# An expert layer's first product: 64 of 256 tokens by gathered rows and dot products on VectorE, 192 tokens left to the dense product on TensorE

## The chip, the cores and the metric

The kernel runs on one core of one Trainium2 chip. The metric is the device time of one execution in microseconds. Every time below comes from the profile, the run times or the trace of the kernel before.

## The reference, cut to what matters

Two blocks follow each other; the changed part is the last layer of the second, an expert layer ("peer") on 256 tokens of width 2048, with 16384 experts. Each of 8 heads picks 16 experts per token, so 128 (token, expert) pairs per token are wanted, out of 16384.

```python
def peer_ffn(x, wq, sub_keys, u, v):
...
        best, pos = lax.top_k(cand, PEER_TOPK)
        expert = jnp.take_along_axis(cidx, pos, axis=-1)
        gate = jax.nn.softmax(best, axis=-1)
        u_sel = u[expert]
        v_sel = v[expert]
        act = jax.nn.gelu(jnp.einsum('td,thkd->thk', xc, u_sel).astype(jnp.float32), approximate=False)
        return jnp.einsum('thk,thkd->td', (gate * act).astype(x.dtype), v_sel)
```

## The kernel before, in words

**The dense way.** The kernel gathers nothing. It multiplies all 256 tokens by all 16384 rows of `u` (the first product), applies gelu, multiplies by a dense matrix of gates that is zero for experts not picked, and multiplies the result by all of `v` (the second product). Both weight matrices, 134 MB each, stream through once.

**A chunk.** Weights come in chunks of 128 x 1024 float32 (512 KB). `split_w` loads one on SP's queue, ScalarE rounds it to its high half (`whi`, line 132), and `sub` (line 121) makes the low half (`wlo`) as the difference, on the engines that `lo_eng[0]` lists in turn. The rings hold 5 raw chunks and 4 of each half. A chunk has 8 blocks of 128 x 128. For each, `mm3` issues two matmuls: the high half against the activations' high and low halves side by side (512 columns, line 145), and the low half against the high half alone (256 columns, line 146). Four chunks make a group of 256 experts; the first product has 64 groups (`u_group`), 256 chunks, and the second (`v_group`) another 256.

**Beside the first product** run three things, called from `mid` once per chunk. `route(0)` and `route(1)` (lines 1017 to 1066, VectorE) find each token's experts and gates for 128 tokens at a time. `gate_prep` (line 1082) makes one-hot matrices on VectorE for a unit of 4 tokens, and `gate_fire` (line 1109) multiplies them on TensorE into that unit's dense gates, which go to `Gd` in DRAM; there are 64 units. After each group, ScalarE copies the cross part (line 183), VectorE adds it (line 190), and gelu goes to `staged` and to `Ad` in DRAM. `fetch` brings `Gd` and `Ad` back, and `w_make` multiplies them into the activations of the second product.

**What sets the order.** The order in which a step stands on its engine is not that of the source alone: a scheduler fixes each engine's list when the program is built, and on the chip each engine takes its list strictly in turn.

Of the kernel before, what the change touches and what calls it, by code (L numbers as in the profile page):

```python
# [18 lines left out]
T = 256  # L19
D = 2048  # L20
KT = 16
# [18 lines left out]
GATES_AT = 16  # L40
SPLIT_FROM = 62
PER_UNIT = 2.3
# [11 lines left out]
def tile_body(ctx: ExitStack, tc: tile.TileContext, xT, vec, dw, w_ccin, w_ccout, w_m1, w_m2,  # L54
              w_p, w_ki, pool_w, rel_bias, bucket, w_o, w_q, subk, w_u, w_v, out):
# [53 lines left out]
    DVE.tensor_scalar(ident, jp[:, :128], 0.0, None, op0=OP.is_equal)  # L109
    iota = const.tile([128, 128], F32, name="iota")  # L110
# [971 lines left out]
    def gate_prep(n):  # L1082

        if n >= SPLIT_FROM:
            o = [pk("oh", [128, 4, 128], F32R, tag=f"oh{i}", bufs=1) for i in range(3)]
            t = slice(4 * n, 4 * n + 4)
            ghi = pk("ghi", [128, 4], F32R, bufs=2)
            glo = pk("glo", [128, 4], bufs=2)
            ACT.activation(ghi, R[:, 2, t], AF.Copy)
            sub(DVE, glo, R[:, 2, t], ghi)  # L1090
            for i in range(4):
                t = slice(4 * n + i, 4 * n + i + 1)
                DVE.tensor_scalar(o[0][:, i], iota, R[:, 0, t], ghi.bitcast(F32)[:, i:i + 1], op0=OP.is_equal, op1=OP.mult)
                DVE.tensor_scalar(o[1][:, i], iota, R[:, 0, t], glo[:, i:i + 1], op0=OP.is_equal, op1=OP.mult)
                DVE.tensor_scalar(o[2][:, i], iota, R[:, 1, t], None, op0=OP.is_equal)
            gates[n] = o
            return
        if not spare:
            more = slot(3, [128, 8, 4, 128], name="hot")
            flat = big.rearrange("p a b -> p (a b)").rearrange("p (n a b) -> p n a b", n=4, a=4)  # L1100
            spare.extend(flat[:, i] for i in range(4))
            spare.extend(more[:, i] for i in range(8))
        o1, o2 = spare[2 * (n % 6):2 * (n % 6) + 2]
        for i in range(4):
            t = slice(4 * n + i, 4 * n + i + 1)
            DVE.tensor_scalar(o1[:, i], iota, R[:, 0, t], R[:, 2, t], op0=OP.is_equal, op1=OP.mult)
            DVE.tensor_scalar(o2[:, i], iota, R[:, 1, t], None, op0=OP.is_equal)
        gates[n] = o1, o2

    def gate_fire(n):  # L1110
        if n % 8 == 0:
            gs.append(slot(4 + n // 8 % 2, [128, 128, 32], name="gs"))
        *o1, o2 = gates.pop(n)
        ps = aux(wide4)
        for i in range(4):
            for j, a in enumerate(o1):
                PE.matmul(ps[:, i], a[:, i], o2[:, i], start=j == 0, stop=j == len(o1) - 1)  # L1117
# [6 lines left out]
    Ad = dram.tile([8, 4, 128, 4, T], F32, name="Ad")  # L1124
    staged = slot(0, [128, 4, 4, T], name="staged")
    wts, last = {}, [None]
    acc = hf
    lnf = Layer()

    def u_group(b, g, mid=None):  # L1130

        q = g // 2

        def ev(o, ps):
            v = wk("nrm", bufs=3)
            last[0] = gathered(ps, v)
            ACT.activation(staged[:, q, o % 4], v, AF.Gelu)  # L1137

        group(w_u[8 * b + g], H, ev, g, mid=mid)
        if g % 2:  # L1140
            nc.gpsimd.dma_start(Ad[b, q], staged[:, q])  # L1141

    def fetch(n):

        if not ring4:
            ring4.append(slot(3, [128, 4, 4, T], name="got"))
            ring4.append(slot(7, [128, 4, 8, 4, 32], name="gt"))
# [6 lines left out]
    def w_make(b, q):  # L1154
# [4 lines left out]
        for i in range(4):  # L1159
            w = got[:, i]  # L1160
            with tc.issue_after(last[0].ins):
                DVE.tensor_tensor(w.rearrange("p (c t) -> p c t", c=8), w.rearrange("p (c t) -> p c t", c=8),  # L1162
                                  gt[:, :, i], OP.mult)
            put_split(wts[b], 4 * q + i, w)
# [25 lines left out]
    with phase("gate"):  # L1190
        lo_eng[0] = [DVE]
        made = [0, 0]
        ripe = [0]

        def routing():
            for b in range(2):
                yield from route(b)
                yield
                yield
                route_end(b)  # L1200

        steps = routing()
        for i in range(64):
            def mid(c, i=i):
                if c in (0, 1, 2):
                    next(steps, None)
                to = int(max(0, min(64, (4 * (i - GATES_AT) + c + 1) / PER_UNIT)))
                while made[1] < ripe[0]:
                    gate_fire(made[1])
                    made[1] += 1  # L1210
                ripe[0] = made[0]
                while made[0] < to:
                    gate_prep(made[0])
                    made[0] += 1
# [53 lines left out]
def lay_out(inp):  # L1268
# [6 lines left out]
    def cols(v):  # L1275
# [27 lines left out]
    o["w_v"] = c(a["peer_v_2"][0].reshape(128, 8, 4, 4, 8, 256).transpose(1, 4, 2, 0, 3, 5))  # L1303
    return o
# [3 lines left out]
         "bucket", "w_o", "w_q", "subk", "w_u", "w_v"]  # L1308
# [16 lines left out]
```

## Time and profile before

| what | value |
|---|---|
| runs | 3055.27, 3045.81, 3044.33 us; median 3045.81 us |
| profiled execution | 3056.73 us, span 3054.9 us |
| TensorE | 2997.2 us busy, 98% of the span |
| VectorE | 2138.3 us, 70% |
| ScalarE | 1576.6 us, 52% |
| GpSimd | 458.3 us, 15% |
| DMA | 608.20 MB, 199 GB/s over the span |

A matmul's listed duration is longer than its share of TensorE's time, since matmuls are pipelined; the distance between starts is its price. A busy share is an average over stages with different limits, so each stage is read by itself.

### The profile page before, as it was taken

The page shows a single profiled execution, that of the slowest core. Times are in us where ns is not written, and L with a number is a line of the kernel's source. Part 1 is how long each engine was busy: PE and PEld are TensorE (multiplying, and loading weights), DVE is VectorE, ACT ScalarE, POOL GpSimd, SP SyncE. Part 2 cuts the span into 40 slices and gives each one's busy share as a digit, 9 for nine tenths or more (in the row PEclk, how much of TensorE's full clock was granted, in tenths as well). Part 3 has the DMA queues.
Part 4 walks back from the last instruction along what each step waited for, and adds up shares of the span by engine and source line. Part 5 has one row for each costly group of instructions (what it writes and reads, how often), then busy time and mean ns, then how long its engine had stood idle before and what let it go on. Part 6 is the DMA issues. An engine that isn't in the chain of part 4 may idle for free.

```text
span 3054.9 us, 47026 instructions
## 1 busy us (share of the span) xinstructions
PE 2997.2 (98%) x17614; PEld 2642.9 (87%) x17614; DVE 2138.3 (70%) x3892; ACT 1576.6 (52%) x2435; POOL 458.3 (15%) x554
## 2 busy tenths in 40 slices
PE   8998999999999999999999999999999999999997
PEld 7997888888888888898888888888888888888886
DVE  7997666455565876767899666666456667676765
ACT  4446554444444644565555555555555445454444
POOL 6883100000000120014400000000100000000014
PEclk9998999999999999999999999999999999999998
DMA  6443655555555555445456666666777777777663
GB/s 224 154 152 113 206 186 186 187 186 187 186 186 186 186 187 182 158 147 179 159 187 214 207 214 227 228 214 215 277 262 245 244 231 243 233 236 241 213 188 109
DMA packets 165045, 608.20 MB, mean 199 GB/s; under 512 B 18232, under 2 KB 20288, under 8 KB 163536
## 3 DMA queue, kind: packets, MB, share of 16 engines
q1 hardware_dynamic: 148992, 533.79, 52.7%
q0 software_dynamic: 15824, 71.41, 7.0%
q8 instruction: 137, 2.24, 0.3%
q14 instruction: 92, 0.75, 0.1%
HBM read 569.40 MB, written 37.24 MB: 199 GB/s over the span
## 4 chain that ended last, share of the span: by engine, by line
PE 91%; DVE 6%; POOL 1%; ACT 1%; issue 0%; DMA 0%; ACTq 0%; DVEq 0%; POOLq 0%
PE mm L145 54%; PE mm L146 28%; DVE aux L433 3%; PE aux L1117 2%; PE mm L363 2%; PE mm L820 0%; PE mm L818 0%; PE mm L819 0%; POOL hf L762 0%; DVE h L471 0%; DVE hf L1239 0%; PE mm L949 0%; PE mm L951 0%; DVE conv L440 0%; PE mm L950 0%
## 5 line engine op out<-in xcount | busy, mean ns | idle before, releaser
L145 PE MATMUL mm<-A,whi 128*128 128x512 f32 x7056 | 2484.3, 396 | 3.6 <-DVE A L121 3.4
L146 PE MATMUL mm<-A,wlo 128*128 128x256 f32 x7088 | 1986.8, 280 | 3.5 <-POOL wlo L121 1.9
L121 DVE TENSOR_TENSOR wlo<-wraw,whi 128x1024 fp32r<-128x1024 f32 x928 | 1139.8, 1233 | 783.7 <-ACT whi L132 782.7
L145 PEld LDWEIGHTS mm<-A,whi 128*128 128x128 f32 x7056 | 1324.0, 188 | 314.6 <-DVE A L121 4.2
L132 ACT ACTIVATE whi<-wraw 128x1024 fp32r<-128x1024 f32 x976 | 1029.6, 1057 | 1042.3 <-PE mm L145 767.4
L146 PEld LDWEIGHTS mm<-A,wlo 128*128 128x128 f32 x7088 | 1339.6, 189 | 4.9 <-POOL wlo L121 2.3
L183 ACT ACTIVATE cross<-mm 128x256 f32<-128x256 f32 x439 | 164.4, 374 | 89.8 <-PE mm L146 89.8
L121 POOL TENSOR_TENSOR wlo<-wraw,whi 128x1024 fp32r<-128x1024 f32 x48 | 117.7, 2463 | 56.1 <-ACT whi L132 56.0
L433 DVE SCALAR_TENSOR_TENSOR aux<-front,dwt,aux 128x256 f32<-128x256 f32 x314 | 125.1, 477 | 0.1
L1141 POOL DMA_DIRECT2D Ad<-staged x32 | 17.2, 536 | 628.2 <-ACT staged L1137 605.7
L1149 POOL DMA_DIRECT2D gt<-Gd x32 | 28.9, 904 | 499.6 <-DVE got L1162 447.4
L231 POOL TENSOR_TENSOR accq<-sq 128x256 f32<-128x256 f32 x5 | 3.9, 777 | 650.8 <-ACT sq L238 650.8
L1137 ACT ACTIVATE staged<-nrm 128x256 f32<-128x256 f32 x128 | 53.1, 415 | 90.7 <-DVE nrm L190 90.7
L363 PE MATMUL mm<-h,raw 128*128 128x256 f32 x448 | 98.0, 379 | 0.0
L190 DVE TENSOR_TENSOR nrm<-mm,cross 128x256 f32<-128x256 f32 x192 | 80.3, 418 | 22.4 <-ACT cross L183 22.4
L363 PEld LDWEIGHTS mm<-h,raw 128*128 128x128 f32 x448 | 84.8, 191 | 11.3
L1119 ACT ACTIVATE gs<-aux 128x512 f32<-128x512 f32 x64 | 72.8, 1138 | 26.8 <-PE aux L1117 26.8
L410 POOL TENSOR_TENSOR nr<-nr 128x256 f32<-128x256 f32 x106 | 78.9, 744 | 18.1 <-ACT nr L409 12.0
L145 PE MATMUL mm<-M,whi 128*128 128x512 f32 x224 | 79.3, 397 | 0.0
L231 POOL TENSOR_TENSOR accq<-sq,accq 128x256 f32<-128x256 f32 x64 | 59.5, 930 | 129.8 <-ACT sq L238 129.5
L146 PE MATMUL mm<-M,wlo 128*128 128x256 f32 x256 | 72.5, 283 | 2.6 <-DVE wlo L121 2.6
L373 PE MATMUL mm<-A,whi 128*128 128x256 f32 x224 | 65.6, 293 | 3.3 <-DVE front L382 2.3
(308 smaller groups left out, 2503.5 us busy)
## 6 DMA issues: line engine op xcount, KB each, us to landing
wraw<-w_m SPq DMA_DIRECT2D x256, 512.0 KB, 3.5
wraw<-w_u SPq DMA_DIRECT2D x256, 512.0 KB, 3.7
wraw<-w_v SPq DMA_DIRECT2D x256, 512.0 KB, 4.3
wraw<-w_p SPq DMA_DIRECT2D x80, 512.0 KB, 3.5
wraw<-w_ccin SPq DMA_DIRECT2D x36, 512.0 KB, 3.6
wraw<-w_ccout SPq DMA_DIRECT2D x32, 512.0 KB, 4.2
wraw<-w_o SPq DMA_DIRECT2D x32, 512.0 KB, 4.3
wraw<-w_q SPq DMA_DIRECT2D x32, 512.0 KB, 3.6
```

Of the source, the lines that this page charges most:

```text
L121: return eng.tensor_tensor(out_, a, b, OP.subtract)
L132: ACT.activation(hi[:, :, :m], raw[:, :, :m], AF.Copy)
L145: PE.matmul(ps, hi[:, k, cs], a, start=kt == 0, stop=False)
L146: PE.matmul(ps[:, :T], lo[:, k, cs], a[:, 0], start=False, stop=kt == KT - 1)
L183: ACT.activation(c, ps[:, T:], AF.Copy)
L190: return DVE.tensor_tensor(dst, ps[:, :T], c, OP.add)
L231: POOL.tensor_tensor(d, ap, self.acc[k], OP.add)
L363: PE.matmul(hold[j][:, :T], raws[c][:, k, blk(j)], src[:, kt], start=kt == 0, stop=kt == KT - 1)
L373: PE.matmul(d, hi[:, k, blk(j)], a[:, 0], start=kt == 0, stop=False)
L410: POOL.tensor_tensor(t, t, p, OP.add)
L433: DVE.scalar_tensor_tensor(d, a, b, add, op0=OP.mult, op1=OP.add)
L1119: ACT.activation(gs[-1][:, :, t:t + 4].rearrange("p c t -> p t c"), ps, AF.Copy)
```

## The change

The first 64 tokens leave the dense product. The selected rows of `u` (a second copy of the weights, `u_rows`, as half rows of 1024 floats) are fetched by indirect DMA from GpSimd's queue, 128 half rows (512 KB) at a time: the two halves of one row of each of 64 tokens. Each fetch is multiplied on VectorE by the tokens' own activations (`Hx`) and summed in one instruction (`dot_rows`). There are 128 fetches and 128 dot products. `weigh` adds the two halves by a matmul, applies gelu and multiplies the gates, so that the dense gates of these tokens hold gate times activation. The dense product runs on 192 tokens: 384 and 192 columns instead of 512 and 256. `gate_prep` uses three instructions of 128 x 512 instead of eight of 128 x 128. And `lo_eng[0]` becomes [DVE, POOL] for both products, so every second chunk's low half is made on GpSimd.

```diff
     def gate_prep(n):
...
+        i = 2 * (len(order) % 2)
+        o1, o2 = (big.rearrange("p a b -> p (a b)")[:, 512 * j:512 * j + 512].rearrange("p (t a) -> p t a", t=4)
+                  for j in (i, i + 1))
+        order.append(n)
+        r = [R[:, c, 4 * n:4 * n + 4, None].to_broadcast(wide4) for c in range(3)]
+        keys = iota[:, None, :].to_broadcast(wide4)
+        DVE.tensor_tensor(o1, keys, r[0], OP.is_equal)
+        DVE.tensor_tensor(o1, o1, r[2], OP.mult)
+        DVE.tensor_tensor(o2, keys, r[1], OP.is_equal)
         gates[n] = o1, o2
...
+    def fetch_rows(j):
...
+        p = pieces[j % 5]
+        got_rows[j] = p
+        POOL.indirect_dma_start(out=p, out_offset=None, in_=u_rows,
+                                in_offset=bass.IndirectOffsetOnAxis(ap=idx[:, j:j + 1], axis=0))
+
+    def dot_rows(j):
+        p = got_rows.pop(j)
+        DVE.tensor_tensor_reduce(out=p, in0=p, in1=Hx, scale=1.0, scalar=0.0, op0=OP.mult, op1=OP.add,
+                                 accum_out=dots[:, j:j + 1])
...
+    def mm_late(ps, hi, lo, k, o, A, kt, fine):
+        a = A[kt // 8][:, kt % 8]
+        PE.matmul(ps[:, :2 * ND].rearrange("p (i t) -> p i t", i=2), hi[:, k, blk(o)], a[:, :, NS:],
+                  start=kt == 0, stop=False)
+        PE.matmul(ps[:, :ND], lo[:, k, blk(o)], a[:, 0, NS:], start=False, stop=kt == KT - 1)
...
     with phase("gate"):
-        lo_eng[0] = [DVE]
+        lo_eng[0] = [DVE, POOL]
...
+        def looking(to):
+            while looked[1] < min(to, 128):
+                dot_rows(looked[1])
+                looked[1] += 1
+                while looked[0] < min(128, looked[1] + 5):
+                    fetch_rows(looked[0])
+                    looked[0] += 1
+            if looked[1] == 128 and not done:
+                done.append(1)
+                weigh()
...
             u_group(i // 8, i % 8, mid)
-            if i == 55:
+            if i == 60:
                 for n in range(4):
                     fetch(n)
-            if i > 55 and i % 2:
-                w_make(0, (i - 56) // 2)
+            if i > 60:
+                w_make(0, i - 61)
+        w_make(0, 3)
```

**Where instructions now stand.** The first place is VectorE in the middle of `route`, with the large comparisons of its first block. `wlo` is a chunk's low half, `nrm` the addition after a group, `z` routing data. Before:

```order
L1041 TENSOR_TENSOR z_14174<-z_14173,z_14174 128x128x15
L190 TENSOR_TENSOR nrm<-mm,cross 128x256
L121 TENSOR_TENSOR wlo<-wraw,whi 128x1024 x2
L1044 TENSOR_REDUCE z_14173<-z_14174 128x128
L190 TENSOR_TENSOR nrm<-mm,cross 128x256
L121 TENSOR_TENSOR wlo<-wraw,whi 128x1024
L1046 TENSOR_TENSOR z_14174<-z_14174 128x128x15
L121 TENSOR_TENSOR wlo<-wraw,whi 128x1024 x2
```

And with the change:

```order
L1049 TENSOR_TENSOR z_14176<-z_14175,z_14176 128x128x15
L1187 TENSOR_TENSOR nrm<-mm,cross 128x192
L1052 TENSOR_REDUCE z_14175<-z_14176 128x128
L1072 TENSOR_REDUCE sm<-z_14175 128x8
L1054 TENSOR_TENSOR z_14176<-z_14176 128x128x15
L1187 TENSOR_TENSOR nrm<-mm,cross 128x192
L129 TENSOR_TENSOR wlo<-wraw,whi 128x1024
L1056 TENSOR_REDUCE z_14175<-z_14176 128x128
```

Between two low halves that VectorE makes there are more routing steps than before, and each of its low halves now stands for two chunks of the product: routing stands between the first 24 chunks, where before it was spread over some 40.

The second place is GpSimd's list during the first product. Before, it holds DMAs alone (`Ad` after every second group, `Gd` after every 8 units):

```order
L1020 CAST z_14173<-z_14173 128x256 x2
L1141 DMA Ad<-staged_15042 128x1024 x10
L1121 DMA Gd<-gs_16885 128x4096
L1141 DMA Ad<-staged_15042 128x1024 x2
L1121 DMA Gd<-gs_17471 128x4096
```

With the change, in the stretch of the dot products (`rows` and `piece` are the five buffers of fetched rows):

```order
L129 TENSOR_TENSOR wlo<-wraw,whi 128x1024
L1149 DMA rows_17127<-u_rows,z_14176 128x1024 x5
L129 TENSOR_TENSOR wlo<-wraw,whi 128x1024
L1149 DMA rows_17127<-u_rows,z_14176 128x1024 x4
L129 TENSOR_TENSOR wlo<-wraw,whi 128x1024
```

VectorE's list in the same stretch is this (the second line of each dot product reads its sum out):

```order
L129 TENSOR_TENSOR wlo<-wraw,whi 128x1024
L1154 ISA rows_17127,z_14176<-rows_17127,state_15043 128x1024
L1154 ISA z_14176 128x1
L1187 TENSOR_TENSOR nrm<-mm,cross 128x192
L1154 ISA rows_17127,z_14176<-rows_17127,state_15043 128x1024
L1154 ISA z_14176 128x1
L1187 TENSOR_TENSOR nrm<-mm,cross 128x192
L1154 ISA rows_17127,z_14176<-rows_17127,state_15043 128x1024
L1154 ISA z_14176 128x1
L1154 ISA rows_17127,z_14176<-rows_17127,state_15043 128x1024
L1154 ISA z_14176 128x1
L129 TENSOR_TENSOR wlo<-wraw,whi 128x1024
```

All 128 dot products stand between 31 low halves of VectorE, so within 62 of the 256 chunks, about four to a pair of chunks; the source asks for one in 1.3 chunks. Nearly all units of gates stand behind them.

## Rows read from the trace of the kernel before

**Rows 1.** The page's head: span, the chain's shares by engine.

```profile
span 3054.9 us, 47026 instructions
...
PE 91%; DVE 6%; POOL 1%; ACT 1%; issue 0%; DMA 0%; ACTq 0%; DVEq 0%; POOLq 0%
```

**Rows 2.** Stretches: us, busy us (x instructions) by engine, PEclk, DMA share, GB/s.

```profile
1545.00:2318.00 773.00, 773.00 (x4620) 683.89 (x4619) 544.81 (x1141) 431.97 (x600) 31.66 (x55) 1.00 0.67 227
1551.00:1670.00 119.00, 119.00 (x685) 104.29 (x684) 118.83 (x259) 63.40 (x91) 3.11 (x6) 1.00 0.64 207
2318.00:3010.00 692.00, 692.00 (x3987) 609.37 (x3986) 478.72 (x733) 344.40 (x502) 72.09 (x83) 1.00 0.70 228
```

**Rows 3.** TensorE in order of time, first product: start us, us, instruction.

```profile
1639.90 0.40 PE L145 MATMUL mm<-A,whi 128*128 128x512 f32 x1
...
1642.72 0.40 PE L145 MATMUL mm<-A,whi 128*128 128x512 f32 x1
```

**Rows 4.** TensorE in order of time: short matmuls with their own weights.

```profile
242.34 0.58 PE L244 MATMUL aux<-ones,conv 128*128 128x1 f32 x4
242.79 0.58 PE L244 MATMUL aux<-ones,sq 128*128 128x1 f32 x4
...
1804.94 1.05 PE L1117 MATMUL aux<-hot 128*128 128x128 f32 x8
1805.75 0.47 PE L145 MATMUL mm<-A,whi 128*128 128x512 f32 x1
...
2184.92 1.01 PE L1117 MATMUL aux<-oh 128*128 128x128 f32 x8
2185.76 0.45 PE L145 MATMUL mm<-A,whi 128*128 128x512 f32 x1
```

**Rows 5.** VectorE in order of time, first product.

```profile
1547.36 0.49 DVE L937 MAX8 z<-s 128x8 f32<-128x128 f32 x2 [1.49 <-ACT s L933]
...
1551.59 0.29 DVE L1024 TENSOR_TENSOR z<-z 128x128 f32<-128x128 f32 x1
...
1569.99 0.42 DVE L190 TENSOR_TENSOR nrm<-mm,cross 128x256 f32<-128x256 f32 x1
1570.33 2.35 DVE L121 TENSOR_TENSOR wlo<-wraw,whi 128x1024 fp32r<-128x1024 f32 x2
1572.60 2.14 DVE L1044 TENSOR_REDUCE z<-z 128x128 f32<-128x1920 f32 x1
```

**Rows 6.** GpSimd's low halves, all: min/median/max ns.

```profile
L121 POOL TENSOR_TENSOR wlo<-wraw,whi x48: 2349/2398/3340, 30.2 to 1532.2; 128x1024 fp32r<-128x1024 f32 x48
```

**Rows 7.** GpSimd and VectorE at once, in order of time; line 282's usual ns.

```profile
1443.74 2.44 POOL L121 TENSOR_TENSOR wlo<-wraw,whi 128x1024 fp32r<-128x1024 f32 x1 [4.84 <-ACT whi L132]
...
1443.90 2.57 DVE L282 TENSOR_TENSOR sq<-ident,t_dr 128x256 f32<-128x256 f32 x1
...
1459.49 1.21 DVE L121 TENSOR_TENSOR wlo<-wraw,whi 128x1024 fp32r<-128x1024 f32 x1
...
1459.87 3.10 POOL L121 TENSOR_TENSOR wlo<-wraw,whi 128x1024 fp32r<-128x1024 f32 x1 [1.66 <-ACT whi L132]
...
1500.83 2.49 POOL L121 TENSOR_TENSOR wlo<-wraw,whi 128x1024 fp32r<-128x1024 f32 x1 [3.87 <-ACT whi L132]
...
1501.00 0.48 DVE L937 MAX8 z<-s 128x8 f32<-128x128 f32 x2
...
L282 DVE TENSOR_TENSOR sq<-ident,t_dr x3: 425/425/2574, 246.4 to 3035.5; 128x256 f32<-128x256 f32 x3
```

**Rows 8.** A stretch at the kernel's start, columns as in the second group.

```profile
10.00:15.00 5.00, 5.00 (x17) 4.11 (x16) 4.26 (x11) 3.97 (x15) 3.11 (x7) 1.00 1.02 410
```

**Rows 9.** GpSimd's DMA issues (ns), and one beside VectorE.

```profile
L1149 POOL DMA_DIRECT2D gt<-Gd x32: 882/904/913, 2205.2 to 2854.5; - x32
...
1640.36 2.29 DVE L1052 TENSOR_TENSOR z<-z,iota 128x2048 f32<-128x2048 f32 x1
...
1640.99 0.53 POOL L1141 DMA_DIRECT2D Ad<-staged  x1 [24.84 <-ACT staged L1137]
```

More of the change, by code (lines that the diff above doesn't have):

```diff
@@ L1121, in gate_fire, with rows_of_tokens, places, weigh @@
             nc.gpsimd.dma_start(Gd[n // 8], gs[-1])
-    Ad = dram.tile([8, 4, 128, 4, T], F32, name="Ad")
-    staged = slot(0, [128, 4, 4, T], name="staged")
+    state = slot(0, [128, 4096], name="state")
+    staged = state[:, :16 * ND].rearrange("p (q o t) -> p q o t", q=4, o=4)
+    Hx = state[:, 3072:]
+    look = z2f[:, 1456:1968].rearrange("p (n r) -> p n r", n=4)
+    idx, dots = look[:, 0].bitcast(U32), look[:, 1]
+    pieces = []
+    def rows_of_tokens(j):
+        c = wk("sq", [128, 2, NS], bufs=4)
+        ACT.activation(c, hf[:, j::8, :NS], AF.Copy)
+        ps = aux()
+        PE.transpose(ps[:, :128], c.rearrange("p a t -> p (a t)"), ident)
+        ACT.activation(Hx[:, blk(j)], ps[:, :128], AF.Copy)
+    def places():
+        tr = zt(0, "tr").rearrange("p (c r) -> p c r", c=3)
+        a, b = look[:NS, 2], look[:NS, 3]
+        DVE.tensor_scalar(b, tr[:NS, 1], 2.0, None, op0=OP.mult)
+        DVE.scalar_tensor_tensor(a, tr[:NS, 0], 256.0, b, op0=OP.mult, op1=OP.add)
+        DVE.tensor_copy(idx[:NS], a)
+        DVE.tensor_scalar(a, a, 1.0, None, op0=OP.add)
+        DVE.tensor_copy(b.bitcast(U32), a)
+        nc.gpsimd.dma_start(idx[NS:], b.bitcast(U32))
+    def fetch_rows(j):
+        if not pieces:
+            pieces.append(pk("piece", [128, 1024], bufs=1))
+        if j in (0, FIRST):
+            rows4 = slot(3 if j else 5, [128, 4, 1024], name="rows4")
+            pieces[1:] = [rows4[:, i] for i in range(4)]
+        p = pieces[j % 5]
[6 more added lines that the diff above has]
+                                 accum_out=dots[:, j:j + 1])
+    def weigh():
+        ps = aux()
+        PE.matmul(ps[:, :NS], dots, fold, start=True, stop=True)
+        g = wk("sq", [128, NS], bufs=4)
+        ACT.activation(g, ps[:, :NS], AF.Gelu)
+        DVE.tensor_tensor(R[:, 2, :NS], R[:, 2, :NS], g, OP.mult)
+    got_rows, order = {}, []
+    Ad = dram.tile([8, 4, 128, 4, ND], F32, name="Ad")
     wts, last = {}, [None]
@@ L1190, in tile_body, with gating @@
     with phase("gate"):
-        lo_eng[0] = [DVE]
+        lo_eng[0] = [DVE, POOL]
         made = [0, 0]
         ripe = [0]
+        looked = [0, 0]
+        late = NS // 4
         def routing():
[L1196 to L1200, printed above, removed]
+            yield from route(0)
+            places()
+            yield
+            yield
+            route_end(0)
+            yield from route(1)
+            yield
+            yield
+            route_end(1)
+        def gating(to):
+            while made[1] < ripe[0]:
+                gate_fire(units[made[1]])
+                made[1] += 1
+            ripe[0] = made[0]
+            while made[0] < to:
+                gate_prep(units[made[0]])
+                made[0] += 1
+        def looking(to):
[8 more added lines that the diff above has]
+                weigh()
+        units = list(range(late, T // 4)) + list(range(late))
+        done = []
         steps = routing()
```

91 lines of the change are left out of this document (42 added, 49 removed).

## The prediction

> **What bounds the kernel now.** I read the head of the page first: TensorE carries 91% of the chain of work that ended last, in a span of 3054.9 us [rows 1]. The change lies in one stage, so the stretches come next [rows 2]. The first product lasts 773 us, and TensorE is busy in 773 of them at a granted clock of 1.00 (2.4 GHz). VectorE is busy 545, GpSimd 32, DMA 0.67. So today each column taken from the matmuls shortens the stage, and VectorE has some 228 us to spare.
>
> The price of the product is the distance between starts. Eight high-half matmuls of 512 columns with their eight low-half ones of 256 take 2.82 us [rows 3], so a block costs 0.3525 and 2048 blocks cost 722 us. A unit of gates costs TensorE 0.81 us [rows 4]; 64 make 52. Together that is 774, the stage.
>
> **TensorE's part, removed.** 384 columns cost 0.235 x 0.75 = 0.176 us. 192 would cost 0.088 by columns. But one-column matmuls with weights of their own come four in 0.45 us (0.112 each), and 128-column ones eight in 0.84 (0.105 each) [rows 4], so a short matmul has a floor. I take 0.105 and keep 0.088 and 0.157 (the 128-column price by columns) as bounds. The second is far, since one column costs no less than 128 here. A block is then 0.281 us (0.264 to 0.333), a chunk of eight 2.25. TensorE alone falls from 773 to 576 + 52 = 628, so 145 us would be gained if nothing else came in.
>
> The Trainium skill, "TensorE: Matmul & The Clock Gate", section "Back-to-back issue gap", gives about 81 ns for each 128-column matmul in a sustained stream with weight loads. By it 192 columns would go at the column price, and the sum below would be some 27 us lower. The 105 ns of this trace decides against it.
>
> **VectorE's part.** These are its prices, by distance of starts. A low half: two in 2.27 us, 1.135 each [rows 5]; 128 of them now, 145 us. An addition: 0.34 at 256 columns [rows 5], some 0.27 at 192; 128, 35 us. A dot product is an operation that the trace lacks. The nearest row reads two 128x1024 arrays and writes one, the low half, so I take 1.2 with the reading out of its sum. Below, 1.135; above, 2.27, should it multiply and add in two passes. 128 of them, 154 us. A gate unit: three instructions of 128x512, each near 0.6 between 0.34 for 256 and 1.135 for 1024; 1.8, 64 units, 115 us. Routing: in its 119 us VectorE is busy throughout [rows 2], and 42 low halves and 21 additions among them leave 64. Each of the two rank heads that stand with it takes 4.2 us [rows 5]. With some 5 for the second product's activations VectorE alone needs some 527 us, still under TensorE's 628.
>
> **GpSimd's part.** A low half takes it 2.40 us [rows 6]; 128 are 307. A DMA issue takes 0.53 to 0.90 [rows 9], so 128 fetches 68 to 115, beside other work.
>
> **Where the two meet.** Earlier in this kernel GpSimd also made low halves. There a VectorE addition of 128x256 from two SBUF arrays, usually 0.425 us, took 2.57 and ended just behind a GpSimd low half that had begun 0.16 before it [rows 7]. The other way round, a GpSimd low half that began during a VectorE one took 3.10 in place of 2.40. A MAX8, with one input, ran beside a GpSimd low half unhindered. So VectorE's instructions with two SBUF arrays (low halves, dot products, gates, the large comparisons) and GpSimd's low halves exclude each other, for the whole instruction. Their times add up: 145 + 154 + 115 + 307 and some 30 of routing are 751 us, in a stage that lasts 773 today. That sum decides, stage by stage, since the dot products are packed into 62 chunks.
>
> **First 24 chunks (routing).** TensorE needs 54. VectorE: 64 + 8.5 + 12 low halves at 1.135 (13.6) + 12 additions (3) = 89. GpSimd's 12 low halves take 29, half of which I let hold VectorE up (14), and buffers filled ahead give 7 back: 96 us.
>
> **Next 16 chunks.** TensorE sets the pace: 16 x 2.25 and two units, 38.
>
> **62 chunks with dot products.** VectorE: dots 154, nine units 16, additions 8, low halves 35: 213. GpSimd's 31 low halves, 74, cannot lie beside them: 287, less 7 to 9 by buffers filled ahead, 280 us. TensorE needs 147. On GpSimd's list a fetch stands ahead of each low half and waits for the dot that frees its buffer, so the low half comes when VectorE could go on; that is why I count it in full. The raw chunks and rows come to 100 MB here (190 pieces of 0.524 MB); at the 410 GB/s that this kernel reaches at its start [rows 8] they take 243 us, hidden under 280.
>
> **Last 154 chunks.** TensorE: 154 x 2.25 + 53 x 0.81 = 389. VectorE and GpSimd in exclusion: 77 x (1.135 + 2.40) + 53 x 1.8 + 21 = 388. Equal demands in two chains with four buffers between them do not overlap perfectly; I give 10 for waits: 399.
>
> **Sum.** 96 + 38 + 280 + 399 = 813, against 773: +40. Transposing the 64 tokens and weighing their sums adds about 2, the late `Gd` fetches behind GpSimd's list some 3. In the second product TensorE is busy 692 of 692 and VectorE 479 [rows 2]; half of its low halves leave VectorE (145 less) and GpSimd's 307 come, 641 even in exclusion. Still under 692, so I give it 2. That is +45 to +47. The profiled execution took 3056.73 us, so the sum makes it 3102; the median of the runs shown is 10.9 lower, so there 3090.
>
> **The rivals.** *Faster: the exclusion costs nothing here.* GpSimd's low halves run in the gaps, as they do beside MAX8 [rows 7]. Then the four stretches are 82 (VectorE alone), 38, 243 (DMA) and 389: 752, so -21 with the same small items at nothing, and 3025; with 192 columns at the column price 3000. For it: the sum of exclusive work is below 773, VectorE has gaps where it waits for ScalarE, and one dot in four or five meets a low half. Against: 2.57 for 0.425, and no idle time on VectorE while dots are queued. It decides if dots and low halves beside a GpSimd low half stay at 1.2.
>
> *Slower: fetches also shut VectorE out.* A plain DMA issue from GpSimd ran in 0.53 us beside a VectorE instruction of two SBUF arrays [rows 9]. But a fetch has row numbers to read from SBUF, and no row shows that. If each of 128 holds the dots up for the 0.53 to 0.90 of an issue, 68 to 115 us come to the third stretch, 92 in the middle: 3182.
>
> The Trainium skill, "SBUF — State Buffer", section "Who interferes with whom", says that a VectorE instruction with two SBUF inputs and a GpSimd instruction that reads SBUF hold the shared port in turn, the other fully blocked. By it a fetch, which reads its row numbers, could exclude dots as a low half does, the 3182 of this rival; the same section infers that issuing a DMA needs the port's other side, which such VectorE instructions leave free. On low halves the trace agrees, 2.57 us for 0.425; on fetches no row here speaks.
>
> *The gathered rows come late.* Rows are 4 KB pieces from scattered places. If DMA gives only its mean rate while busy (227 GB/s at 0.67, 339 [rows 2]), 100 MB take 295 us, 15 more than VectorE and GpSimd: 3105.
>
> *The dot product takes two passes.* 128 x 1.07 more, 137 us: 3227. Against it: every two-array instruction here makes one pass.
>
> **The numbers.** My own course has 0.50, the faster rival 0.24, fetches that exclude 0.15, late rows 0.08, two passes 0.03. A change of 0.5%, 15 us, is about what can be told from none. Faster by more than that (below 3031): three quarters of its rival, 0.18. Within it: the rest of that rival, 0.06, and 0.08 of my own (the column price, and fewer meetings of the two engines). Slower: 0.68. The likeliest gives 3090; its own range is 3050 to 3125. The range of 8 in 10 takes in the faster rival down to 3020 and the fetch rival up into its dearer half, 3190.
>
> **What would show it.** Eight blocks start 2.25 us after the last eight (2.1 if columns set the price) where halves are ready. The stretch of dots lasts some 280 us, with TensorE near half busy and the dots four to a pair of chunks. Dots near 1.2 us, but 3 to 4 when a GpSimd low half began before them; GpSimd's low halves above 2.4. DMA in that stretch stands near 360 GB/s; at 340 with dots waiting for rows, the third rival is right. In the last stretch TensorE is nearly full, with small gaps behind GpSimd's `wlo`. Dots that all take 1.2 with GpSimd busy beside them would make the course wrong towards faster; dots that are longer while only a fetch is on GpSimd, towards 3182. Wrong too would be low halves on VectorE longer than 1.2 in the second product, with TensorE waiting there.

## The result, and the profile after

The changed kernel took 3216.52 us (median of 4 runs, 3202.24 to 3227.41) against 3045.07 before: a ratio of 1.0553, 95% interval 1.0505 to 1.0601. It is slower, as forecast, but by 171 us where 45 were forecast, and outside the range. The profiled execution has a span of 3225.6 us against 3054.9 [rows 1]. The medians below leave out one run of experiment 1 that took 5692.99 us in the slow state.

Stretches of the profile after (us, busy us by PE, PEld, DVE, ACT, POOL, granted clock, DMA share, GB/s), cut where the forecast's four stretches end; the last row is what follows the first product:

```profile
1545.00:1643.00 98.00, 66.83 (x384) 62.60 (x383) 94.47 (x232) 35.38 (x58) 40.64 (x21) 0.88 0.45 150
1643.00:1676.00 33.00, 30.64 (x204) 30.38 (x204) 19.57 (x20) 18.09 (x32) 16.08 (x9) 0.95 0.71 239
1676.00:2025.00 349.00, 231.36 (x1088) 213.12 (x1087) 251.77 (x342) 87.40 (x137) 251.62 (x164) 0.75 0.83 288
2025.00:2459.00 434.00, 416.09 (x2937) 410.92 (x2937) 336.77 (x335) 244.49 (x373) 215.57 (x115) 0.99 0.74 256
2459.00:3225.00 766.00, 734.62 (x4166) 637.34 (x4164) 505.34 (x652) 362.58 (x541) 392.61 (x227) 0.98 0.65 208
```

| stretch | forecast | measured |
|---|---|---|
| first 24 chunks, routing | 96 | 98 |
| until the first dot product | 38 | 33 |
| the 62 chunks with dot products | 280 | 349 |
| the rest of the first product | 399 | 434 |
| from its end to the end (737 before) | 742 to 744 | 767 |

TensorE was busy throughout the first product before [rows 2]; now it is busy 231 of 349 us among the dots. Three engines are two thirds to three quarters busy there, DMA 0.83, and none is full. What they wait for stands in the groups by line of that stretch (line, engine, operation, busy us and mean ns, then idle before it and what ended that):

```profile
L1154 DVE CUSTOM_DVE_ANT_0 rows<-rows,state 128x1024 f32<-128x1024 f32 x102 | 153.4, 1525 | 52.6 <-DMA rows<-u_rows,z 52.0
L1154 DVE CUSTOM_DVE_ANT_0 piece<-piece,state 128x1024 f32<-128x1024 f32 x26 | 39.8, 1531 | 42.5 <-DMA piece<-u_rows,z 42.5
...
L1149 POOL DMA_INDIRECT rows<-u_rows,z x98 | 136.0, 1388 | 35.6 <-issue 21.5 <-DVE z L1154 8.4 <-DVE nrm L1187 3.6
...
L1149 POOL DMA_INDIRECT piece<-u_rows,z x25 | 34.7, 1386 | 34.2 <-DVE z L1154 15.8 <-DVE nrm L1187 12.2 <-issue 3.5
...
L1177 PE MATMUL mm<-A,wlo 128*128 128x192 f32 x507 | 160.4, 316 | 108.2 <-POOL wlo L129 61.2 <-DVE wlo L129 46.9
```

VectorE stood idle 95 us for fetched rows, which no term of the forecast's sum held. A fetch took GpSimd 1.39 us on average, with 0.3 more ahead of most of them, where I had 0.53 to 0.90. 123 fetches with that make 196 us; with 31 low halves (75) GpSimd's list comes to some 270 of the 349 us. TensorE waits 108 us for low halves.

Both meetings of the two engines can be seen one by one. VectorE (start, us):

```profile
1862.42 4.08 DVE L1154 CUSTOM_DVE_ANT_0 rows<-rows,state 128x1024 f32<-128x1024 f32 x1 [1.46 <-DMA rows<-u_rows,z]
...
1866.44 1.21 DVE L1154 CUSTOM_DVE_ANT_0 rows<-rows,state 128x1024 f32<-128x1024 f32 x1
...
1890.82 1.22 DVE L1154 CUSTOM_DVE_ANT_0 rows<-rows,state 128x1024 f32<-128x1024 f32 x1 [0.28 <-DMA rows<-u_rows,z]
```

And GpSimd:

```profile
1862.10 0.94 POOL L1149 DMA_INDIRECT rows<-u_rows,z  x1 [0.30 <-issue]
1863.06 2.35 POOL L129 TENSOR_TENSOR wlo<-wraw,whi 128x1024 fp32r<-128x1024 f32 x1
1866.79 1.70 POOL L1149 DMA_INDIRECT rows<-u_rows,z  x1 [1.37 <-DVE z L1154]
...
1890.53 0.95 POOL L1149 DMA_INDIRECT rows<-u_rows,z  x1 [0.30 <-issue]
```

The dot at 1862.42 took 4.08 us and ended 1.09 behind the low half of 1863.06: exclusion, as forecast. By the rows this dot had begun 0.64 before the low half. Twelve dots began before the low half that they met, and five of them still ended 1.09 behind it, all five begun beside a fetch; what decides who goes first, the rows don't show. The dot at 1890.82 ran beside a fetch and took its usual 1.22. The fetch at 1866.79, begun while a dot ran, took 1.70 in place of 0.95.

Over all 128 of each: dots that overlap only a fetch take 1.22 us (78 of them), those that overlap a low half 2.57 on average (29, so 39 us more in all). Fetches that begin while no two-array instruction of VectorE runs take 0.95 (median of 29), those that begin during one 1.69 (median of 99), and eight in ten of these end 0.82 to 0.92 us after that instruction does. So the fetch waits for the dot, not the dot for the fetch.

One piece of the stretch is a case of its own. From 1742 to 1798 only one buffer (`piece`) is in use, since the other four change their place in memory there. VectorE, and then GpSimd:

```profile
1748.60 1.23 DVE L1154 CUSTOM_DVE_ANT_0 piece<-piece,state 128x1024 f32<-128x1024 f32 x1 [4.68 <-DMA piece<-u_rows,z]
...
1755.67 1.23 DVE L1154 CUSTOM_DVE_ANT_0 piece<-piece,state 128x1024 f32<-128x1024 f32 x1 [4.70 <-DMA piece<-u_rows,z]
```

```profile
1750.11 1.73 POOL L1149 DMA_INDIRECT piece<-u_rows,z  x1 [2.26 <-PE mm L1177]
1751.85 2.40 POOL L129 TENSOR_TENSOR wlo<-wraw,whi 128x1024 fp32r<-128x1024 f32 x1
...
1757.18 1.70 POOL L1149 DMA_INDIRECT piece<-u_rows,z  x1 [2.93 <-DVE z L1154]
```

Each dot waits for a whole round of dot, issue and landing, 5.5 to 7.2 us.

In the second product VectorE's additions have become dear, and the matmuls a little. Groups by line, after and (L1181) before, then a stretch of 40 us of each:

```profile
L1234 DVE TENSOR_TENSOR hf<-hf,cross 128x256 f32<-128x256 f32 x110 | 137.5, 1250 | 3.8
```

```profile
L1181 DVE TENSOR_TENSOR hf<-hf,cross 128x256 f32<-128x256 f32 x110 | 47.3, 430 | 3.7
```

```profile
2700.00:2740.00 40.00, 40.00 (x228) 34.69 (x227) 26.48 (x31) 18.60 (x26) 20.82 (x11) 1.00 0.77 238
```

```profile
2690.00:2730.00 40.00, 40.00 (x233) 35.24 (x232) 28.59 (x45) 19.93 (x30) 2.89 (x4) 1.00 0.72 237
```

TensorE is full in both, yet issues 228 matmuls where it issued 233: a block costs 0.3533 us in place of 0.3467, some 14 us over 2048 blocks.

### The profile page after: what moved, and what is told of

It reads as the page before. It is cut to its first block, busy times and chain, and to the rows that moved or that the text cites. A ratio compares the mean times of both kernels' runs of the same rounds, so it can differ in the third digit from the quotient of the medians.

```text
span 3225.6 us, 47205 instructions
## 1 busy us (share of the span) xinstructions
PE 2987.7 (93%) x17624; PEld 2683.2 (83%) x17624; DVE 2298.0 (71%) x3569; ACT 1533.3 (48%) x2449; POOL 1259.7 (39%) x939
## 4 chain that ended last, share of the span: by engine, by line
PE 67%; DVE 16%; issue 7%; POOL 5%; DMA 3%; ACT 2%; POOLq 0%; ACTq 0%; DVEq 0%
PE mm L153 37%; PE mm L154 19%; DVE wlo L129 3%; DVE aux L441 3%; PE mm L1175 3%; POOL wlo L129 2%; DVE z L1099 2%; PE mm L1177 1%; POOL rows L1149 1%; PE mm L371 1%; DMA rows<-u_rows,z 1%; ACT whi L140 1%; DMA piece<-u_rows,z 1%; DVE rows L1154 1%; DVE z L1098 1%
## 5 line engine op out<-in xcount | busy, mean ns | idle before, releaser
L153 PE MATMUL mm<-A,whi 128*128 128x512 f32 x5008 | 1776.0, 400 | 7.0 <-DVE A L129 6.3
L154 PE MATMUL mm<-A,wlo 128*128 128x256 f32 x5040 | 1417.1, 281 | 10.7 <-POOL wlo L129 8.3
L129 DVE TENSOR_TENSOR wlo<-wraw,whi 128x1024 fp32r<-128x1024 f32 (+1 forms) x672 | 923.4, 1376 | 625.9 <-ACT whi L140 625.2
L129 POOL TENSOR_TENSOR wlo<-wraw,whi 128x1024 fp32r<-128x1024 f32 x304 | 751.7, 2475 | 575.7 <-ACT whi L140 539.7
L1177 PE MATMUL mm<-A,wlo 128*128 128x192 f32 x2048 | 557.1, 272 | 157.6 <-DVE wlo L129 85.2
L1175 PE MATMUL mm<-A,whi 128*128 128x384 f32 x2048 | 674.5, 393 | 11.5 <-ACT whi L140 11.5
L1154 DVE CUSTOM_DVE_ANT_0 rows<-rows,state 128x1024 f32<-128x1024 f32 x102 | 153.4, 1525 | 52.6 <-DMA rows<-u_rows,z 52.0
L1149 POOL DMA_INDIRECT rows<-u_rows,z x102 | 140.9, 1382 | 36.6 <-issue 22.6
L191 ACT ACTIVATE cross<-mm 128x256 f32<-128x256 f32 x311 | 116.8, 376 | 67.5 <-PE mm L154 67.5
L1234 DVE TENSOR_TENSOR hf<-hf,cross 128x256 f32<-128x256 f32 x110 | 137.5, 1250 | 3.8
```

Of the source, the lines that this page charges most:

```text
L129: return eng.tensor_tensor(out_, a, b, OP.subtract)
L153: PE.matmul(ps, hi[:, k, cs], a, start=kt == 0, stop=False)
L154: PE.matmul(ps[:, :T], lo[:, k, cs], a[:, 0], start=False, stop=kt == KT - 1)
L191: ACT.activation(c, ps[:, T:], AF.Copy)
L1149: POOL.indirect_dma_start(out=p, out_offset=None, in_=u_rows, in_offset=bass.IndirectOffsetOnAxis(ap=idx[:, j:j + 1], axis=0))
L1154: DVE.tensor_tensor_reduce(out=p, in0=p, in1=Hx, scale=1.0, scalar=0.0, op0=OP.mult, op1=OP.add, accum_out=dots[:, j:j + 1])
```

## The experiments

Names in the table: U is the first product, the dots' stretch runs from the first to the last dot product, the tail from the end of U to the end of the program, all from the profiled executions. The ratio is to the kernel before, by its runs on the same chip. The scheduler lays each kernel out anew: by the low halves that begin in it, the dots' stretch covers 61 chunks in the changed kernel and in experiments 1 and 9, 56 in 5, 52 in 8 and 48 in 6. So U says more than the stretch. The part ahead of U, which no experiment edits, took 1528 to 1545 us in these profiles, so small differences of the totals say little.

| kernel | median us | ratio (95%) | U | dots | tail |
|---|---|---|---|---|---|
| before | 3045.07 | | 773 | | 737 |
| the change | 3216.52 | 1.0553 (1.0505 to 1.0601) | 917 | 348 | 767 |
| 1 low halves on VectorE | 3135.87 | 1.0288 (1.0233 to 1.0342) | 854 | 314 | 739 |
| 2 dots spread | 3159.28 | 1.0354 (1.0311 to 1.0397) | 867 | 581 | 767 |
| 3 both | 3054.42 | 1.0023 (1.0000 to 1.0047) | 770 | 503 | 740 |
| 4 before, alternating halves | 3097.76 | 1.0158 (1.0119 to 1.0197) | 800 | | 760 |
| 5 one set of buffers | 3207.95 | 1.0488 (1.0446 to 1.0530) | 903 | 314 | 766 |
| 6 no fetches | 3142.64 | 1.0301 (1.0271 to 1.0330) | 843 | 239 | 765 |
| 7 no dots | 3200.15 | 1.0490 (1.0460 to 1.0520) | 898 | | 767 |
| 8 half the bytes | 3212.51 | 1.0512 (1.0480 to 1.0544) | 917 | 325 | 767 |
| 9 plain DMAs | 3176.86 | 1.0420 (1.0383 to 1.0456) | 883 | 314 | 767 |
| 10 three buffers | 3269.63 | 1.0731 (1.0698 to 1.0765) | 966 | 385 | 768 |
| 11 second product on VectorE | 3205.56 | 1.0511 (1.0473 to 1.0548) | 916 | 349 | 753 |
| 12 both, more evenly | 3047.55 | 0.9996 (0.9978 to 1.0014) | 761 | 551 | 754 |
| 13 the same, gelu later | 3050.08 | 0.9987 (0.9968 to 1.0006) | 761 | 552 | 741 |
| 14 the same, gates on ScalarE | 3090.41 | 1.0139 (1.0115 to 1.0163) | 804 | 580 | 740 |

**1. All low halves on VectorE.**

```diff
-        lo_eng[0] = [DVE, POOL]
+        lo_eng[0] = [DVE]
```

> The changed kernel, but VectorE makes all low halves of both products (GpSimd keeps only fetches and DMAs). Theory A (exclusion: GpSimd's low halves and VectorE's two-array instructions take turns, and that is most of the 170 us): the stretch of dot products goes from 349 us to about 264 (128 dots at 1.28, 63 low halves at 1.135, 8 gate units), the last stretch from 438 to 405, the second product back by its 25: about 3095 in all. Theory B (packing: dots stand too close, and fetched rows come late through five buffers and GpSimd's list): low halves hardly matter, the stretch of dots stays above 310, about 3150 to 3180. Theory C (pace: the matmuls of the second product run at 0.353 us a block instead of 0.347 whoever makes low halves): the second product keeps 14 of its 25 us.

81 us came back by the medians, between the theories A and B (92 by the profiled executions, 63 of them in U and 28 in the tail). In the last stretch of U, TensorE is now full, where it stood idle 18 us of 434 in the changed kernel:

```profile
1983.00:2380.00 397.00, 396.71 (x2850) 396.46 (x2850) 297.66 (x390) 250.30 (x356) 18.83 (x33) 1.00 0.76 263
```

But the dots' stretch only fell to 314 us, with 70 us of waits for rows left in it. Exclusion is one cause, and not the whole.

**2. Dots spread over 42 groups.** Each dot is tied to come after the last addition of the group before.

```diff
-                dot_rows(looked[1])
+                with tc.issue_after(last[0].ins):
+                    dot_rows(looked[1])
```

> The changed kernel, but each dot product is tied to come after the last addition of the group before, so that 3 of them stand in every group of four chunks over 42 groups, in place of all 128 within 62 chunks; GpSimd still makes every second low half. Theory A: the sum of exclusive work stays, 751 us and more, so the first product comes to 760 to 800 instead of 918: 3070 to 3100. Theory B: the wait for rows goes (95 us of VectorE's time now), TensorE is the bound again with 643 us and some 50 in the routing stretch: 700, about 2980 to 3000. If neither, it stays near 3216.

3159, more than either theory said, because I had added exclusive work up over the whole product. It has to be added up per stretch: a group of four chunks now holds 2 x (1.135 + 2.40) of low halves, 3.05 dots at 1.23, 0.54 of additions and 1.14 gate units at 1.8, together 13.4 us; 42 groups make 563. Measured, 581. No dot waited for rows any more. Exclusion, by its full price, is thus shown where packing is gone.

**3. Both edits.**

> Both edits: dots spread over 42 groups, and all low halves on VectorE. VectorE then has 291 + 154 + 115 + 64 + 35 + 14 = 673 us of work in the first product, TensorE 643, so the first product should take about 700 to 715. Theories A and B both give about 2975 to 2995, faster than the kernel before; A says that it beats the spread kernel with GpSimd's low halves by 80 or more, B that the two are within 20. Theory C adds up to 14 if the second product runs at the slower pace.

3054, 105 us under the spread kernel, as theory A had it, but not the 2975 to 2995 that both theories gave. All dots take 1.21 to 1.23 us:

```profile
L1154 DVE CUSTOM_DVE_ANT_0 rows<-rows,state x102: 1211/1218/1226, 1666.7 to 2167.6; 128x1024 f32<-128x1024 f32 x102
```

So taking the low halves off GpSimd is worth 81 us with the dots packed and 105 with them spread, removing the packing 57 or 81. Some 28 of the 81 and of the 105 lie in the second product, which the same edit changes. Yet 770 us for U is no gain over 773, though TensorE's own work is some 640: VectorE is busy 443 of the 504 us that this view of the dots' stretch covers, and the rest goes into its waits.

```profile
1665.00:2169.00 504.00, 450.60 (x3043) 437.92 (x3042) 443.23 (x643) 254.98 (x381) 206.38 (x149) 0.97 0.92 339
```

**4. The kernel before, with alternating low halves.**

```diff
-        lo_eng[0] = [DVE]
+        lo_eng[0] = [DVE, POOL]
```

> The kernel before, but low halves of both products alternate between VectorE and GpSimd. Theory A: nothing to pay for where TensorE is the bound with slack on both engines (exclusive work about 145 + 307 + 35 in 773): within 10 us of before, 3045 to 3055. Theory C: the second product may run at the slower pace, 14 more: 3060. A rival, that GpSimd's low halves alone cost what the second product lost (25): 3070 and VectorE's additions there grow from 0.43 to 1.25 us as in the changed kernel.

54 us slower than the kernel before on that chip, more than any of the three said. TensorE, full before, stands idle 16.5 us in the routing stretch for low halves; U takes 27 more and the tail 22 to 23.

```profile
L146 PE MATMUL mm<-A,wlo 128*128 128x256 f32 x318 | 91.7, 288 | 16.5 <-DVE wlo L121 14.7 <-POOL wlo L121 1.7
```

The alternation alone, without any token leaving the dense product, costs about a third of the change's 171.

**5. One set of buffers.** The four row buffers keep their place; some gates go elsewhere.

```diff
-        if j in (0, FIRST):
-            rows4 = slot(3 if j else 5, [128, 4, 1024], name="rows4")
+        if j == 0:
+            rows4 = slot(5, [128, 4, 1024], name="rows4")
...
```

> The changed kernel, but the fetched rows keep one set of five buffers to the end (the gates that needed that place go elsewhere), so that no stretch is left in which a single buffer serves ten fetches in a row (56 us for 9 dots in the changed kernel, 1742 to 1798). Theory B1 (that round trip is a cost of its own): those ten chunks take some 30 us, the total falls by 20 to 30, to 3187 to 3197. Theory A (only exclusion counts): within 5 us of 3216.

The one-buffer piece is gone and the dots' stretch is 35 us shorter, but it covers five chunks fewer, and the total fell by 9, which the intervals don't part from nothing. That piece was not the cause by itself.

**6. No fetches.** The dots read what lies in their buffers.

```diff
-        POOL.indirect_dma_start(out=p, out_offset=None, in_=u_rows,
-                                in_offset=bass.IndirectOffsetOnAxis(ap=idx[:, j:j + 1], axis=0))
+        if j < 5 or FIRST <= j < FIRST + 5:
+            ACT.activation(p, Hx, AF.Copy)
```

> The changed kernel without the 128 fetches: the dot products read what lies in the five buffers (written once by ScalarE), so the sums of those 64 tokens are not the reference's. Low halves still alternate. Theory A: the stretch of dots stays at what exclusion makes of it, 154 + 10 for reading out + 74 of GpSimd's low halves + 60, about 280 to 300 in place of 349: 3150 to 3165. Theory B (late rows and GpSimd's list are all of it): the dots overlap with the product, the stretch falls towards VectorE's own 225: 3090 or less.

74 us came back, all of it in U, as theory A said. VectorE is then full in the dots' stretch (234 of 238 us). With 48 chunks in it the work in turn, 128 x 1.23 + 24 x 3.53, is 242, and 256 with 24 additions and three gate units:

```profile
1667.00:1905.00 238.00, 160.38 (x836) 150.84 (x834) 234.11 (x312) 72.53 (x110) 72.57 (x31) 0.82 0.34 119
```

**7. No dots.** A copy of one column frees each buffer.

```diff
-        DVE.tensor_tensor_reduce(out=p, in0=p, in1=Hx, scale=1.0, scalar=0.0, op0=OP.mult, op1=OP.add,
-                                 accum_out=dots[:, j:j + 1])
+        DVE.tensor_copy(dots[:, j:j + 1], p[:, :1])
```

> The changed kernel without the 128 dot products: each is replaced by a copy of one column on VectorE that frees the buffer, so the sums of those 64 tokens are not the reference's. Fetches stay, packed as closely as before. If GpSimd's list sets the stretch by itself (128 fetches at 0.95 + 0.30 us = 160, 31 low halves 75), it takes 235 to 250: 3105 to 3115. If dots set it, it falls to TensorE's 145 or DMA's 243 at 410 GB/s; that 243 and GpSimd's 235 are too close to be told apart by the time, but by DMA's rate they can: near 410 GB/s with GpSimd waiting, or GpSimd busy throughout.

Only 16 us came back, far less than either part of the expectation. The fetches alone hold U at 898. They run from 1583 to 1970, beside 79 chunks, so the first of them lie under routing here. VectorE, which now has little to do, waits 241 us of that for rows, 145 for the four large buffers and 96 for the fifth, and GpSimd waits for VectorE to free buffers:

```profile
L1154 DVE COPY z<-rows 128x1 f32<-128x1 f32 x101 | 15.1, 152 | 145.2 <-DMA rows<-u_rows,z 145.2
...
L1154 DVE COPY z<-piece 128x1 f32<-128x1 f32 x26 | 4.0, 152 | 95.8 <-DMA piece<-u_rows,z 95.8
...
L1149 POOL DMA_INDIRECT piece<-u_rows,z x26 | 31.5, 1210 | 73.1 <-DVE z L1154 44.6 <-DVE nrm L1186 24.3 <-DMA z<-z 3.1
```

The expectation had overlooked the rounds through the buffers.

**8. Half the bytes of each fetch.**

```diff
-        POOL.indirect_dma_start(out=p, out_offset=None, in_=u_rows,
...
+        POOL.indirect_dma_start(out=p[:, :512], out_offset=None, in_=u_rows.rearrange("r (h c) -> (r h) c", h=2),
```

> The changed kernel with every fetch cut to half its bytes (512 of 1024 floats a row, rows of other experts; the other half of each buffer holds what ScalarE wrote once), so the sums of those 64 tokens are not the reference's. Number of fetches, of dots and buffers stay. If bytes set the stretch (DMA stands at 0.88 of its engines there, 306 GB/s), 33 MB less take 90 to 100 us less of DMA and it comes near the kernel without fetches: 3140 to 3160. If the number of fetches sets it (GpSimd's list, round trips through five buffers), it stays within 20 of the changed kernel: 3195 to 3216.

4 us, and U did not move: bytes don't set it. DMA's share in the dots' stretch fell from 0.83 to 0.59, yet VectorE still waited 84 us for rows (95 before). The rival of late rows by DMA's rate falls.

```profile
1678.00:2003.00 325.00, 195.32 (x924) 182.75 (x923) 240.66 (x320) 75.19 (x120) 246.66 (x157) 0.76 0.59 192
```

**9. Plain DMAs in place of fetches.**

```diff
-        POOL.indirect_dma_start(out=p, out_offset=None, in_=u_rows,
-                                in_offset=bass.IndirectOffsetOnAxis(ap=idx[:, j:j + 1], axis=0))
+        nc.gpsimd.dma_start(p, u_rows[128 * j:128 * j + 128])
```

> The changed kernel with each of the 128 fetches as a plain DMA of 128 consecutive rows on the same queue of GpSimd: same bytes, same buffers, no row numbers to read, so the sums of those 64 tokens are not the reference's. If GpSimd's list sets the stretch of dots (128 fetches at 1.39 + 0.30 us and 31 low halves at 2.44 are 292 of its 349 us), an issue at 0.55 to 0.90 takes 100 to 140 us out of the list, and the stretch falls to what VectorE and GpSimd need in turn, 250 to 290: 3140 to 3165. If the round trip through five buffers sets it (dot, issue, landing after 3 to 5 us), only a little is gained: 3190 to 3216.

40 us came back, between the two, with the dots beside as many chunks as in the changed kernel. The issue of a plain DMA is the same beside a dot as alone:

```profile
L1149 POOL DMA_DIRECT2D rows<-u_rows x102: 528/531/565, 1425.6 to 1971.9; - x102
L1149 POOL DMA_DIRECT2D piece<-u_rows x26: 528/545/562, 1541.8 to 1967.8; - x26
...
  DVE z L1153: 96.9, 72
```

GpSimd's list has become short, and it now waits 97 us for dots to free a buffer, while VectorE still waits 61 for rows. List and round trip are two sides of one loop. How much of the 40 is the shorter issue, and how much the wait of the issue for dots, this run doesn't part.

**10. Three buffers** in place of five, in the kernel of experiment 5.

```diff
-        p = pieces[j % 5]
+        p = pieces[j % 3]
...
```

> The kernel with one set of buffers to the end (3208), but three buffers in place of five. If GpSimd's list sets the stretch, within 15 us of 3208. If the round trip of a buffer does, the stretch of 311 us grows by up to two thirds of itself where it binds: 3270 and more.

62 us more, so with three the round trip binds. That it binds in part with five too follows from the waits of experiments 7 and 9.

**11. The second product alone on VectorE.**

```diff
     with phase("out"):
+        lo_eng[0] = [DVE]
```

> The changed kernel, but in the second product alone VectorE makes all low halves, as before the change. The time from the end of the first product to the end of the program was 737 us before and is 767 with the change. If GpSimd's low halves there are the cause, it goes back to 737 to 753 (the spread between the two paces of the matmuls) and the total falls by 15 to 30: 3187 to 3202. If what the first product leaves behind is the cause (late gates, a lower clock at the start), it stays at 767: 3216.

The tail fell from 767 to 753, and the additions went back to 0.43 us. But the matmuls stayed at 228 in 40 us:

```profile
2700.00:2740.00 40.00, 40.00 (x228) 34.67 (x228) 28.31 (x47) 19.93 (x30) 2.92 (x4) 1.00 0.72 235
```

So of the tail's 30 us about 13 are GpSimd's low halves and 14 the slower pace, and the slower pace comes with all low halves on VectorE too. Whether low halves on GpSimd favour it stays open: all nine profiles that have them in the second product ran at it, and two of the seven that don't. The medians differ by 11, less than the runs scatter; the split rests on the profiles (experiments 12 and 13 show the 13 to 14 of the pace once more, 754 and 741).

**12. Spread more evenly** (dots in groups 7 to 55, gates from group 12, the last ones in groups 56 to 60), on top of 3.

```diff
-LOOK_AT = 10
-PER_LOOK = 1.3
+LOOK_AT = 7
+PER_LOOK = 1.5
...
```

> Spread dots and all low halves on VectorE, and spread more evenly: dots from group 7 to 55 at 2.7 a group (in place of group 11 to 52 at 3), gates from group 12 on at one unit in 3.55 chunks, the last 16 units in groups 56 to 60. VectorE's work per group of four chunks falls from 11.6 to some 10.8 us beside TensorE's 10.2. Expected: 15 to 30 us under the kernel without this edit, 3025 to 3040, a little faster than the kernel before. If VectorE's waits on the loop addition, gelu, high half, low half (54 us) set the pace rather than its work, no gain: 3054.

U fell by 9, to 761; no difference from the kernel before.

**13. Each gelu put off until the next addition**, on top of 12.

```diff
             last[0] = DVE.tensor_tensor(v, ps[:, :ND], c, OP.add)
-            ACT.activation(staged[:, q, o % 4], v, AF.Gelu)
+            flush()
+            pend.append((b, q, o, v))
...
```

> The evenly spread kernel with all low halves on VectorE, and each gelu of the first product put off until the next addition stands, so that ScalarE doesn't hold the next chunk's high half behind an addition that waits in VectorE's list. If that loop (addition, gelu, high half, low half) costs what VectorE waits for high halves in the stretch of dots (54 us of 480 in the spread kernel), the first product falls from 760 to 710 to 735, the total to 3000 to 3025, faster than the kernel before. If VectorE's own work sets the pace (673 us in all), a gain of under 10: 3040 to 3047.

U stayed at 761. VectorE's waits for high halves did not move either (65.0 and 64.2 us between 1660 and 2180), nor ScalarE's waits for additions ahead of a gelu (230 and 229 us). So the edit did not loosen the loop that it was made for, and whether that loop costs what was expected is not decided by it.

**14. Gates multiplied on ScalarE**, on top of 12.

```diff
-        DVE.tensor_tensor(o1, o1, r[2], OP.mult)
+        for i in range(4):
+            ACT.activation(o1[:, i], o1[:, i], AF.Copy, scale=R[:, 2, 4 * n + i:4 * n + i + 1])
```

> The evenly spread kernel with all low halves on VectorE, and the multiplication of the one-hot matrices by the gates moved from VectorE to ScalarE (four activations of 128x128 with a scale a unit). VectorE loses 64 x 0.6 = 38 us of its 673, ScalarE gets about 64 x 1.1 = 70 in a stage where it is half idle. If VectorE's work is what keeps the first product at 760 against TensorE's 643, 15 to 35 us go: 3012 to 3032, faster than the kernel before. If ScalarE's place in the loop (high halves behind other work) sets it, no gain or a loss: 3047 or more.

43 us slower. VectorE's busy time between 1660 and 2180 fell by 46 us, but TensorE did less there too (3119 matmuls for 3284). VectorE's wait for high halves grew from 65.0 to 107.4 us:

```profile
L129 DVE TENSOR_TENSOR wlo<-wraw,whi 128x1024 fp32r<-128x1024 f32 x174 | 208.5, 1222 | 107.4 <-ACT whi L140 105.6 <-ACT z L1100 1.7
```

So it is not VectorE's work alone that keeps U at 761: what stands ahead of a high half in ScalarE's list counts too. A rival that no run tests is DMA: in this stretch of experiment 12 it stood at 0.93 of its engines (343 GB/s), and ScalarE waited 16 us for raw chunks. No kernel here beats the one before by more than its measurement can tell.

## Why the prediction was right or wrong

**Routing, right.** 98 us for 96; VectorE is busy 94 of them.

**TensorE's price, right by luck: two errors cancelled.** At full clock a block starts 0.284 to 0.290 us after the last, 0.286 in the middle (0.281 forecast). The rows show its two parts:

```profile
1861.22 0.36 PE L1175 MATMUL mm<-A,whi 128*128 128x384 f32 x1
1861.42 0.25 PE L1177 MATMUL mm<-A,wlo 128*128 128x192 f32 x1
1861.51 0.37 PE L1175 MATMUL mm<-A,whi 128*128 128x384 f32 x1
```

The low half takes 0.09, the column price, and not the floor of 0.105 that I took from 128-column matmuls; the high half takes 0.20 and not 0.176. The Trainium skill, "TensorE: Matmul & The Clock Gate", section "Back-to-back issue gap", was nearer for the low half, since its 81 ns for 128 columns set no floor above 0.09; going by columns misses the high half either way. The 27 us that I said the column price would take off were not there by the sum's own terms: VectorE's and GpSimd's 388 stood beside TensorE's 389 in the last stretch.

**Exclusion, right in kind.** Dots take one pass (1.225 us for 1.2) and take turns with GpSimd's low halves. Experiments 2 and 6 show its price per stretch within 7% (563 for 581, 256 for 239). In the changed kernel itself only 29 dots met a low half, which cost them 39 us of the 74 that I counted, since VectorE was waiting for rows for much of the rest.

**"128 fetches 68 to 115, beside other work", wrong.** This is the step that failed. I took the fetch's price from plain issues and let it lie under the dots. It costs 1.39 us on average and 0.3 ahead of it, some 200 us on GpSimd's list beside 75 of low halves, and five buffers make dot, fetch and landing one loop. Without fetches 74 us are back (experiment 6), and half the bytes bring nothing (8). That is about the 69 us by which the dots' stretch missed. The rival "fetches shut VectorE out" had this size (68 to 115) with the wrong party waiting, so its nearer total, 3182, would have been luck. The Trainium skill, "SBUF — State Buffer", section "Who interferes with whom", holds here in the direction that I did not cost: the GpSimd instruction that reads SBUF is the one that waits, 1.69 us for 0.95. The other direction, which its exclusive lock would give too, is not there: 50 dots that began during a fetch took 1.21 to 1.25 us. A plain DMA, with no row numbers to read, issues in 0.53 either way, as its remark on the port's other side would have it. That it is the reading of row numbers that waits is argued, not shown: the two kinds of issue may differ in more.

**The rest of the first product, mis-sized.** 434 for 399: TensorE's own work is 416 in place of 389 (156 chunks and 55 units instead of 154 and 53, at the dearer block, make some 402; some blocks ran at the lower clock, and the rest is not taken apart), and waits are 18 in place of 10. Experiment 1 takes the waits away.

**The second product, mis-sized.** "I give it 2", and it lost 30: 13 by GpSimd's low halves and 14 by the matmuls' pace (experiment 11), which the sum did not have at all. The sum of exclusive work was below TensorE's 692, as forecast, and TensorE is full in the middle of the product. But at its two ends there is no slack: TensorE stands idle 4 and 28 us there, against 2 and 20 in experiment 11. At the end GpSimd has its share of the last layer norm as well, and one low half behind it costs TensorE a wait of 6.4 us:

```profile
PE mm L154 <- POOL wlo L129: 6.4, 1, 6.4
```

**The other rivals, refuted.** Dots did not stay at 1.2 beside a low half, as the faster rival needs, and they took one pass, not two. Rows did come late, as the late-rows rival says, but not by DMA's rate: DMA stood at 288 GB/s, below both rates that I had used, and half the bytes changed nothing (experiment 8).

## What to carry to other kernels

Cost a gather at the price of its issuing engine beside the very instructions that use the rows, and look at it as a loop (issue, landing, use, buffer free) that runs through a given number of buffers, not as bytes. Where two engines exclude each other, add their work up stretch by stretch as the scheduler has packed it: the sum over the whole product (751 under 773) said that all was nearly well, the sum over the dots' stretch did not. Work moved to an idle engine is not free when that engine stands in a loop through strictly ordered lists: with GpSimd's low halves (experiment 4) and with ScalarE's gates (14) VectorE had less work, and the kernels were slower by 54 and 43 us.

## What the runs showed of the hardware

An indirect fetch on GpSimd takes 0.95 us when it begins beside no VectorE instruction with two SBUF arrays, and 1.69 (median) when it begins during one, which itself is not slowed (1.22). It then ends 0.81 to 0.94 us after that instruction, in the changed kernel as in experiments 1, 2, 3 and 8. A plain DMA issue takes 0.53 in both cases (experiment 9).

The same stream of 512- and 256-column matmuls runs at one of two paces for as long as nothing interrupts it: 0.3467 or 0.3533 us a block. In the kernel before, the first product goes from the one to the other at an interruption by three short transposes (1622) and changes after gate units; the second product runs at 0.3467 throughout there and at 0.3533 in the changed kernel. Experiments 11 and 12 had the slower one with VectorE making all low halves, 1, 3, 13 and 14 the faster. Ahead of the first product, in code that the experiments share, the same stream ran at 0.3467 in eight of the 16 profiles and at 0.3533 in the other eight (between 520 and 900 us); the eight reach the first product at 1528 to 1535 us, the others at 1541 to 1545. What chooses stays open.

The granted clock fell to 0.75 of full speed in the dots' stretch, where TensorE stops between chunks for low halves, and a block there often took 0.53 us in place of 0.29. No run tells what that cost by itself; in the spread kernel (experiment 2) the clock stood at 0.94 in that stretch and the time was still that of the work in turn.
